# An output projection with seven quarter products for eight, and its operand's sums made one stage earlier

## The chip, the cores and the metric

The kernel runs on one core of one Trainium2 chip. The metric is the device time of one execution in microseconds (us). In the rows that are shown, PE is TensorE (matmul), PEld its weight load, DVE is VectorE, ACT is ScalarE, POOL is GpSimd and SP is SyncE, which issues most DMAs; ACT issues the rest from its own queue (ACTq).

## The reference

One layer of a streaming encoder for 1024 prompt tokens and 64 sample tokens of width 1024. Two attention branches (sb and cb) feed a gated merge and an output projection; the change touches only what stands behind the attention, in the reference's `merge`:

```python
b_sb = (o_sb.reshape(lead + (WIDTH_SB,)) * jax.nn.silu(z_sb)) @ w_proj_sb      # 512 -> 1024
b_cb = (o_cb.reshape(lead + (WIDTH_CB,)) * jax.nn.silu(z_cb)) @ w_proj_cb      # 512 -> 1024
h = jax.nn.sigmoid(g_sb) * b_sb + jax.nn.sigmoid(g_cb) * b_cb
return x + h @ w_out                                                           # 1024 x 1024
```

All is float32.

## The kernel before

TensorE works on float32 in a rounded form (fp32r). So each operand is split into a high part (a rounded copy, made by ACT) and a low part (the difference, made by DVE or POOL), and each product is three matmuls: high x high, high x low, low x high. A weight block `wraw` becomes `whi` and `wlo` in this way (`Weights.split`, L117; ACT for the high part, POOL for the low).

Every engine works through its own queue in program order, which the code writes out by hand; an instruction waits for its operands and for the buffers that it overwrites, and what stands behind it on its engine waits with it.

The stages that matter here come last. While the cb attention runs, the sb branch's projection fills TensorE; its results, times the gates, lie in `tb` (two tiles `tbt`, named x..1). Then comes the **cb projection** (`proj_units("cb")`, L822 to L875): 24 units, one for each block of 128 features (`u`, 0 to 7) and each of three token ranges (`CH`: 384, 384 and 320 columns). A unit is 12 matmuls into a PSUM tile. DVE multiplies it by the gate (L870) and adds `tb` (L871), ACT rounds the sum h to its high part (L872), and DVE and POOL in turn make the low part (L873). The order of units is `u` 0 and 1 through the three ranges, then 2 and 3, and so on.

The **output projection** (L1177 to L1202) goes over four blocks of 256 columns of `w_out` and, in each, over nine token tiles. A tile is 24 matmuls of 256 columns (8 k-slices of three), with h as the stationary operand and the weight moving; DVE adds x (L1201) and ACT's queue stores y (L1202). The tile of the 64 sample rows (`t == 8`) has high and low parts of h side by side in `hs`, so that 16 matmuls do for it, and `fold` adds the two halves.

An earlier stage of the kernel (the q and k projections, L600 to L642) already multiplies two by two blocks with seven products instead of eight; its sums of x are made by `make_t` (L326).

Of the kernel before, what the change touches and what calls it, by code (L numbers as in the profile page):

```python
# [8 lines left out]
F32 = mybir.dt.float32  # L9
# [8 lines left out]
KT = 8  # L18
# [14 lines left out]
def hybrid_step_kernel(ctx: ExitStack, tc: tile.TileContext, x_prompt, x_sample, c_sbk, c_sbv, c_cbk, c_cbv,  # L33
# [106 lines left out]
    units += [("ev_act", 5120 + 128 * j, (AF.Copy, d_g["cb"][j])) for j in range(KT)]  # L140

# [4 lines left out]
    with ExitStack() as ph:  # L146
# [178 lines left out]

        def make_t(tm, pool):  # L326

            x = lambda s, h, k, c: xhl[s][h][:, k, c * HF:(c + 1) * HF].bitcast(F32)

            def put(n, k, src):  # L330
                A.activation(tm[n][0][:, k], src, AF.Copy)
                V.tensor_tensor(out=tm[n][1][:, k], in0=src, in1=tm[n][0][:, k].bitcast(F32), op=OP.subtract)

            def sub(a, b, k):
                d = pool.tile([128, HF], F32, name="d")
                V.tensor_tensor(out=d, in0=x(0, *a[:1], k, a[1]), in1=x(0, *b[:1], k, b[1]), op=OP.subtract)
                V.tensor_tensor(out=d, in0=d, in1=x(1, *a[:1], k, a[1]), op=OP.add)
                V.tensor_tensor(out=d, in0=d, in1=x(1, *b[:1], k, b[1]), op=OP.subtract)
                return d

            def less(h, c, d, k):
                e = pool.tile([128, HF], F32, name="d")
                V.tensor_tensor(out=e, in0=x(0, h, k, c), in1=d, op=OP.subtract)
                V.tensor_tensor(out=e, in0=e, in1=x(1, h, k, c), op=OP.add)
                return e

            def sums_of(k):
                d = sub((0, 1), (0, 0), k)
                yield 0, k, d
                d = less(1, 1, d, k)  # L350
                yield 1, k, d
                yield 3, k, less(1, 0, d, k)
                yield 2, k, sub((1, 1), (0, 1), k)

            held = None
            for k in range(4):
                for got in sums_of(k):
                    if held:
                        put(*held)
                    held = got  # L360
                    yield
            put(*held)
# [385 lines left out]
    def run_fill():  # L748
# [25 lines left out]
        with tc.tile_pool(name="tbp", bufs=1, side="right") as tbp:  # L774
            g = proj_units("sb", tbp, 4)
            next(g)
            next(g)
            for i, v in enumerate(g):
                yield v
                og_step(i % 3 == 2)  # L780
# [9 lines left out]
    def hid(s, u):  # L790
        return xk(s, u) if u < 4 else late["h"][s][:, u - 4]

    def load_proj(i):
        if i < 8:
            w = w_proj_sb if i < 4 else w_proj_cb
            c = (i % 4) * 256
            W.load(("p", i), wpool, w[:, c:c + 256].rearrange("(k p) n -> p k n", p=128), [128, 4, 256])
# [24 lines left out]
    def proj_units(b, pool, ng):  # L822
        gts = {}
        order = [(2 * i + uu, ci) for i in range(KT // 2) for ci in range(3) for uu in range(2)]

        def load_g(x):
            if x < len(order):
                u, ci = order[x]
                a, e = CH[ci]
                gts[x] = pool.tile([128, 384], F32, name="gt", bufs=ng)  # L830
                A.dma_start(gts[x][:, :e - a], d_g[b][u][:, a:e])

        def sig(x):
            if b == "cb" and x < len(order):
                a, e = CH[order[x][1]]
                A.activation(gts[x][:, :e - a], gts[x][:, :e - a], AF.Sigmoid)

        for x in range(ng - 1):
            load_g(x)
# [5 lines left out]
        for x, (u, ci) in enumerate(order):  # L845
            i = u // 2 + (0 if b == "sb" else 4)
# [3 lines left out]
            cw = slice((u % 2) * 128, (u % 2) * 128 + 128)  # L850
# [269 lines left out]
    for ci in range(3):  # L1120
        load_og("cb", ci, late["y"])
        if ci == 1:
            next(g)
# [108 lines left out]
```

## Time and profile before

| | |
|---|---|
| median of three runs | 1026.25 us (1025.65 to 1027.78) |
| the profiled execution | 1026.4 us, of it 1024.6 us from the first to the last instruction |
| granted TensorE clock, mean | 0.998 |
| PE busy | 997.4 us (97%) |
| DVE, ACT, POOL busy | 620.6, 460.4 and 294.3 us |
| cb projection | about 875 to 923 us |
| output projection | about 923 to 1022 us |

A timeline row gives the start and length in us, engine, line, operation, `out<-in`, shape, and in brackets the idle time ahead of it with what ended it. The columns of the other views are told where they are shown.

### The profile page before, as it was taken

The numbers are of one execution on the slowest core, as the hardware profiler recorded it, in microseconds if no ns is written. First come the engines' busy times: TensorE is split into PE (matmuls) and PEld (weight loads), VectorE is DVE, ScalarE is ACT, GpSimd is POOL, SyncE is SP. The second block draws the span as 40 slices with busy tenths as digits, with TensorE's granted clock in tenths as the row PEclk, the third lists the DMA queues.
The fourth block names the chain that finished last, engine by engine and source line by source line (L and its number), as shares of the span: only waits on it lengthen the run. The fifth ranks groups of instructions, "written<-read, shape, count | busy, mean of one in ns | idle before, by whom it ended". The sixth has DMA issues, their size and how long they took to land.

```text
span 1024.6 us, 20312 instructions
## 1 busy us (share of the span) xinstructions
PE 997.4 (97%) x7608; PEld 951.5 (93%) x7608; DVE 620.6 (61%) x1219; ACT 460.4 (45%) x1064; POOL 294.3 (29%) x321
## 2 busy tenths in 40 slices
PE   5999999999999999999999999999999999999998
PEld 5999999999999999988898889898988898999998
DVE  5456663894354554189888877566667674674111
ACT  5544443343343433276676666544445433552000
POOL 3276662205344543211111101110102211453110
PEclk9999999999999999999999999999999999999999
DMA  6726567424555332696566554665656833654322
GB/s 221 229 97 213 181 243 260 136 89 139 173 172 170 118 97 76 177 239 183 139 165 165 151 145 127 183 193 156 177 156 204 236 100 116 202 164 146 108 94 72
DMA packets 174516, 164.22 MB, mean 160 GB/s; under 512 B 34961, under 2 KB 160785, under 8 KB 174289
## 3 DMA queue, kind: packets, MB, share of 16 engines
q1 hardware_dynamic: 157648, 145.08, 47.8%
q10 hardware_dynamic: 16768, 17.83, 5.7%
q8 instruction: 60, 0.98, 0.4%
q14 instruction: 40, 0.32, 0.1%
HBM read 104.14 MB, written 58.72 MB: 159 GB/s over the span
## 4 chain that ended last, share of the span: by engine, by line
PE 89%; DMA 3%; DVE 3%; ACT 2%; issue 1%; POOL 1%; SPq 0%; ACTq 0%; DVEq 0%; POOLq 0%
PE acc L450 18%; PE acc L755 16%; PE b L619 15%; PE acc L861 9%; PE o L1019 7%; PE pt L980 6%; PE z L929 3%; PE z L928 3%; PE acc L1197 3%; PE acc L1196 3%; PE acc L1195 3%; DVE kp L948 1%; DMA out_dram<-kos 1%; DMA wrawx<-in_w_in_dram 1%; DMA ot<-d_osb 1%
## 5 line engine op out<-in xcount | busy, mean ns | idle before, releaser
L114 POOL TENSOR_TENSOR wlo<-wraw,whi 128x1024 fp32r<-128x1024 f32 x35 | 85.6, 2445 | 281.6 <-ACT whi L107 242.7
L755 PE MATMUL acc<-xh,wlo 128*128 128x384 f32 (+1 forms) x384 | 130.7, 340 | 0.0
L755 PE MATMUL acc<-xh,whi 128*128 128x384 f32 (+1 forms) x384 | 130.2, 339 | 0.0
L755 PE MATMUL acc<-xl,whi 128*128 128x384 f32 (+1 forms) x384 | 128.6, 335 | 0.0
L948 DVE TENSOR_TENSOR_SCAN kp<-kp,imp 64x576 f32<-64x576 f32 (+8 forms) x72 | 102.7, 1427 | 21.7 <-ACT kp L931 21.5
L980 PE MATMUL pt<-ident,be 128*128 128x128 f32 (+2 forms) x608 | 89.6, 271 | 6.6 <-DVE wT L991 3.3
L938 ACT ACTIVATE be<-be,sm 128x640 f32<-128x640 f32 (+5 forms) x72 | 50.7, 704 | 95.4 <-DVE sm L934 95.4
L989 ACT ACTIVATE wT<-pt 128x512 f32<-128x512 f32 (+3 forms) x130 | 63.5, 502 | 53.2 <-PE pt L980 53.0
L980 PEld LDWEIGHTS pt<-ident,be 128*128 128x128 f32 (+2 forms) x608 | 68.7, 140 | 17.9 <-issue 6.4
L450 PE MATMUL acc<-whi,xh 128*128 128x256 f32 x256 | 74.7, 294 | 0.0
L755 PEld LDWEIGHTS acc<-xh,whi 128*128 128x128 f32 x384 | 72.7, 189 | 1.6
L755 PEld LDWEIGHTS acc<-xh,wlo 128*128 128x128 f32 x384 | 72.5, 189 | 1.1
L755 PEld LDWEIGHTS acc<-xl,whi 128*128 128x128 f32 x384 | 72.3, 188 | 0.9
L450 PE MATMUL acc<-wlo,xh 128*128 128x256 f32 x256 | 71.2, 280 | 0.0
L450 PE MATMUL acc<-wlox,xh 128*128 128x256 f32 x256 | 71.2, 280 | 0.0
L450 PE MATMUL acc<-whi,xl 128*128 128x256 f32 x256 | 71.2, 280 | 0.0
L450 PE MATMUL acc<-whix,xh 128*128 128x256 f32 x256 | 71.2, 280 | 0.0
L450 PE MATMUL acc<-whix,xl 128*128 128x256 f32 x256 | 71.1, 280 | 0.0
L949 DVE TENSOR_TENSOR be<-be,kp 64x576 f32<-64x576 f32 (+8 forms) x72 | 60.3, 837 | 9.6
L931 ACT ACTIVATE kp<-z 128x384 f32<-128x384 f32 (+6 forms) x112 | 54.2, 484 | 24.7 <-PE z L929 23.2
L1019 PE MATMUL o<-wT,vp 128*64 128x256 f32 (+1 forms) x608 | 65.2, 356 | 0.0
L1019 PEld LDWEIGHTS o<-wT,vp 128*64 128x64 f32 x608 | 41.4, 136 | 23.1 <-issue 7.1
(240 smaller groups left out, 2919.4 us busy)
## 6 DMA issues: line engine op xcount, KB each, us to landing
wraw<-in_w_in_dram SPq DMA_DIRECT2D x35, 512.0 KB, 4.3
wrawx<-in_w_in_dram SPq DMA_DIRECT2D x13, 512.0 KB, 4.4
sq<-d_qsbT SPq DMA_DIRECT2D x32, 192.0 KB, 4.6
sq<-d_qcbT SPq DMA_DIRECT2D x32, 192.0 KB, 4.1
xt<-in_x_prompt_dram SPq DMA_DIRECT2D x8, 512.0 KB, 6.1
d_kcbT<-hl SPq DMA_DIRECT2D x8, 512.0 KB, 4.5
d_qcbT<-hl SPq DMA_DIRECT2D x8, 512.0 KB, 5.1
d_ksbT<-hl SPq DMA_DIRECT2D x16, 256.0 KB, 2.6
```

The source lines that it names most:

```text
L114: (eng or G).tensor_tensor(out=l, in0=raw, in1=h[:].bitcast(F32), op=OP.subtract)
L450: TE.matmul(ps, x, w, start=m == 0, stop=m == len(steps) - 1)
L619: TE.matmul(ps[:, :m], w[:, hl_, k], right[s](x)[:, k, a:b], start=s < 3 and k == 0 and e == 0, stop=k == 3 and e == 2, skip_group_check=s ...
L755: TE.matmul(ps[:, :b - a], w[:, k], xk(x, k)[:, a:b], start=k == 0 and n == 0, stop=k == KT - 1 and n == 2)
L861: TE.matmul(ps[:, :n], w[:, p, cw], g[:, a:e], start=p == 0 and m == 0, stop=p == NPAIR - 1 and m == 2)
L931: A.activation(kp[:r, x:y], z[:r, :m], AF.Sigmoid, scale=-0.125)
L938: A.activation(be[:r, :n], be[:r, :n], AF.Exp, bias=kp[:r, j:j + 1], scale=-1.0, accum_out=kp[:r, 2:3])
L948: V.tensor_tensor_scan(kp[:r, n - 1::-1], kp[:r, n - 1::-1], im[:, ::-1], 0.0, op0=OP.mult, op1=OP.add)
L949: V.tensor_tensor(out=be[:r, :n], in0=be[:r, :n], in1=kp[:r, 1:n + 1], op=OP.mult)
L980: TE.transpose(pt[:kr, x, :r], be[:r, kb * 128:kb * 128 + kr], ident[:r, :r])
L989: A.activation(w[:, sl:sl + m, q0:q0 + r], pt[:, :m, :r], AF.Copy)
L1019: TE.matmul(o[hd * 64:hd * 64 + 64, c0:c1], vv[:kr, kb, hd * 64:hd * 64 + 64], wT[b, p, j, hd, s // 4][:kr, s % 4, c0:c1], start=si == 0, ...
```

## The change

The output projection is regrouped. `w_out` is taken as two pairs of 256-column blocks; with h cut in two by features (512 and 512) and by tokens (512 and 512), each pair is a 2 x 2 by 2 x 2 block product, done with seven quarter products. A quarter product is 4 token tiles x 4 k-slices x 3 matmuls of 256 columns. Four of the seven left operands are sums of quarters of h (`th0` to `th3`, each with a high and a low part); the four sums of weight blocks are made for each pair. The order of products is `OP_ = [0, 3, 1, 2, 4, "b", 5, 6]`, where `"b"` is a block that only the sample rows need. Products 0, 3 and 6 take h itself, product 1 takes `th1`, product 2 `th0`.

The sums of h are made during the cb projection. Its units now go in the order `u` 0 and 4, 1 and 5, 2 and 6, 3 and 7. The product with the gate stays on DVE (now L891), the addition goes to POOL for all 24 units and writes h over `tb` (L892), ACT rounds one unit later and DVE makes the low part three units later (`keep_h`, L913). From the ninth unit on, one step of `sums_h` (L923, L928) follows each unit: a subtraction of 512 columns, its rounding on ACT and its low part, for one k-slice after the other. The last k-slice's sums stand behind product 0 in the code.

The core of the diff:

```diff
-                t2 = gt
-                hh, hlo = hid(0, u)[:, a:e], hid(1, u)[:, a:e]
-                V.tensor_tensor(out=t2[:, :n], in0=ps[:, :n], in1=gt[:, :n], op=OP.mult)
-                V.tensor_tensor(out=t2[:, :n], in0=t2[:, :n], in1=tb(u)[:, a:e], op=OP.add)
-                A.activation(hh, t2[:, :n], AF.Copy)
-                (G if x % 2 else V).tensor_tensor(out=hlo, in0=t2[:, :n], in1=hh.bitcast(F32), op=OP.subtract)
-            load_g(x + ng - 1)
+                h = tb(u)
+                V.tensor_tensor(out=gt[:, :n], in0=ps[:, :n], in1=gt[:, :n], op=OP.mult)
+                G.tensor_tensor(out=h[:, a:e], in0=gt[:, :n], in1=h[:, a:e], op=OP.add)
+                keep.append((u, a, e))
+                if len(keep) > 3:
+                    keep_h(1, *keep.pop(0))
+                if len(keep) > 1:
+                    keep_h(0, *keep[-2])
+                if x > 7:
+                    next(late["t"][(x - 2) // 6 - 1], None)
+            load_to(x + ng)
...
+    def sums_h(k):
+        x = lambda h, c: tb(k + 4 * h)[:, 512 * c:512 * c + 512]
+        d = {}
+        def step(n, p, q):
+            d[n] = late["hp"].tile([128, 512], F32, name="d", bufs=2)
+            V.tensor_tensor(out=d[n], in0=p, in1=q, op=OP.subtract)
+            A.activation(late["tm"][n][0][:, k], d[n], AF.Copy)
+        def low(n):
+            h, l = (late["tm"][n][s][:, k] for s in range(2))
+            V.tensor_tensor(out=l, in0=d[n], in1=h.bitcast(F32), op=OP.subtract)
+        step(0, x(0, 1), x(0, 0))
+        step(1, x(1, 1), d[0])
+        yield
+        low(0)
+        step(3, x(1, 0), d[1])
+        yield
+        low(1)
+        step(2, x(1, 1), x(0, 1))
+        yield
+        low(3)
+        yield
+        low(2)
...
+    for _ in g:
+        pass
+    prep_o(1)
+    keep_h(0, *keep[-1])
+    while keep:
+        keep_h(1, *keep.pop(0))
...
+    load_ow((0, 0, 1), ow1, "qraw", 2)
+    load_ow((0, 1, 1), ow1, "qraw", 2)
+    for _ in late["t"][2]:
+        pass
+    t3 = late["t"][3]
...
+    for i in range(2):
...
+        for q, s in enumerate(OP_):
+            n = 8 * i + q
+            for m in {0: (), 1: (3,), 2: (4, 5)}.get(n, (n + 3,)):
+                prep_o(m)
...
+            for c in range(2) if s != "b" else ():
+                if s < 3:
+                    bank[OB[s], c] = psB.tile([128, 2, 256], F32, name=f"b{OB[s]}{c}")
+                ps = bank[OB[s], c]
+                for t in range(2):
+                    ts_ = slice((2 * c + t) * 128, (2 * c + t) * 128 + 128)
+                    for k in range(4):
+                        for e, (xs_, wt_) in enumerate(((0, wh), (1, wh), (0, wl))):
+                            TE.matmul(ps[:, t], left[s](xs_)[:, k, ts_], wt_[:, k], start=s < 3 and t == k == e == 0,
+                                      stop=k == 3 and e == 2, skip_group_check=s > 2 or t > 0)
+                p = ps[:]
+                if s == 0:
+                    A.activation(s1[c], p, AF.Copy)
+                    if n == 0 and c == 1:
+                        for _ in t3:
+                            pass
...
+            if n == 0:
+                prep_o(2, V)
```

`prep_o` splits a weight block or a sum of blocks: the sums for product 1 (`ws`) on POOL in the first pair, the high part on ACT, the low part on POOL but for product 1's of the first pair, which is DVE's (the last line). The `qraw` loads take memory that the cb projection's operand `og` held. The gate loads of the cb branch now come behind the last loads and roundings of its `og`, and go to eight buffers. Its weights are loaded as two halves of 128 columns.

DVE's queue at the end of the cb projection and the start of the output. Before, the last units (`gt` products, sums, low parts `hlo`) and then the output's y:

```order
L870 TENSOR_TENSOR gt<-acc,gt 128x384
L871 TENSOR_TENSOR gt<-gt,xl_10321 128x384
L870 TENSOR_TENSOR gt<-acc,gt 128x320
L871 TENSOR_TENSOR gt<-gt,xl_10321 128x320
L873 TENSOR_TENSOR hlo<-gt,hh 128x320
L870 TENSOR_TENSOR gt<-acc,gt 128x320
L871 TENSOR_TENSOR gt<-gt,xl_10321 128x320
L1175 COPY hs<-xl_141 128x4x64
L1175 COPY hs<-hlo 128x4x64
L1201 TENSOR_TENSOR y<-acc,xr 128x256 x4
```

Now, the last twelve rows up to the first y; ahead of them stand the last gate product and the last low parts of h. `xh_10320` and `xl_10321` are the two tiles of h, `d` is a sum of h, `th..l` its low part, `wloo` the low part of product 1's weight:

```order
L1265 TENSOR_TENSOR hs<-xl_10321,hs 128x4x64
L928 TENSOR_TENSOR th2l<-d,th2h 128x512
L923 TENSOR_TENSOR d<-xh_10320 128x512
L923 TENSOR_TENSOR d<-xl_10321,d 128x512
L928 TENSOR_TENSOR th0l<-d,th0h 128x512
L923 TENSOR_TENSOR d<-xl_10321,d 128x512
L928 TENSOR_TENSOR th1l<-d,th1h 128x512
L923 TENSOR_TENSOR d<-xl_10321,xh_10320 128x512
L928 TENSOR_TENSOR th3l<-d,th3h 128x512
L928 TENSOR_TENSOR th2l<-d,th2h 128x512
L1237 TENSOR_TENSOR wloo<-ws_12020,whio 128x1024
L1360 TENSOR_TENSOR xh_12016<-b_11948,xr 128x512
```

Between the last gate product and the first y there were two copies; now there are sixteen instructions: low parts of h, the rest of the third k-slice's sums, the whole of the fourth's, and the weight's low part.

POOL's queue over the last units. Before, low parts of h between low parts of weights:

```order
L873 TENSOR_TENSOR hlo<-gt,hh 128x320
L114 TENSOR_TENSOR wlo<-wraw,whi 128x1024
L873 TENSOR_TENSOR hlo<-gt,hh 128x384 x2
L873 TENSOR_TENSOR hlo<-gt,hh 128x320
L114 TENSOR_TENSOR wlo<-wraw,whi 128x1024
L114 TENSOR_TENSOR wlox<-wrawx,whix 128x1024
```

Now an addition for every unit, and then the two sums for product 1 (`ws_12018`, `ws_12020`) between low parts:

```order
L892 TENSOR_TENSOR xh_10320<-ot,xh_10320 128x384
L892 TENSOR_TENSOR xl_10321<-ot,xl_10321 128x384
L892 TENSOR_TENSOR xh_10320<-ot,xh_10320 128x320
L892 TENSOR_TENSOR xl_10321<-ot,xl_10321 128x320
L1237 TENSOR_TENSOR wlo<-wraw,whi 128x1024
L1220 TENSOR_TENSOR ws_12018<-qraw 128x1024
L1228 TENSOR_TENSOR ws_12020<-ws_12018,wraw 128x1024
L1237 TENSOR_TENSOR wloo<-ws_12018,whio 128x1024
```

The additions came from DVE, and the output's first weights no longer follow the low parts directly.

More of the change, by code (lines that the diff above doesn't have):

```diff
@@ new lines, in hybrid_step_kernel @@
+    late["o"] = prep_o
+    g = proj_units("cb", late["tbp"], 8)
+    for ci in range(3):
+        load_og("cb", ci, late["y"])
+        fill((40, 24, 100000)[ci])
+        if ci == 2:
+            next(g)
+            next(g)
+            late["h"][1] = [xpool.tile([128, 4, T], F32R, name=f"x{s}0") for s in "hl"]
+        make_og("cb", ci)
+    for _ in g:
[4 more added lines that the diff above has]
+        keep_h(1, *keep.pop(0))
+    m4.close()
+    late["tbx"].close()
```

345 lines of the change are left out of this document (223 added, 122 removed).

## The prediction

> **What bounds the kernel now.** I read the page first, then the busy time by stage, then the chain that ended last, and then the timelines of DVE and POOL.
>
> ```profile
> PE 997.4 (97%) x7608; PEld 951.5 (93%) x7608; DVE 620.6 (61%) x1219; ACT 460.4 (45%) x1064; POOL 294.3 (29%) x321
> 875.00:923.00 48.00, 48.00 (x294) 48.00 (x293) 35.87 (x55) 26.94 (x51) 26.23 (x18) 1.00 0.54 168
> 923.00:1022.00 99.00, 97.98 (x831) 97.58 (x829) 24.67 (x54) 12.16 (x20) 17.72 (x9) 1.00 0.34 107
> ```
>
> The first row is the whole span. The other two are stages, with columns window, length, then busy time of PE, PEld, DVE, ACT, POOL, clock, DMA share and rate. TensorE is full in both: the second branch's projection (875 to 923) and the output projection (923 to 1022). The difference is the rest: the output stage needs little of DVE and POOL, but in the projection they are busy for 35.9 + 26.2 = 62 us out of 48. The change loads that stage further.
>
> ```profile
> L861 PEld LDWEIGHTS acc<-og,whi x192: 187/188/188, 875.1 to 922.2; 128*128 128x128 f32 x192
> 922.53 0.31 PE L861 MATMUL acc<-og,wlo 128*128 128x320 f32 x1
> L1195 PE MATMUL acc<-whi,xh x128: 277/280/283, 922.7 to 1019.4; 128*128 128x256 f32 x128
> 1012.04 0.28 PE L1195 MATMUL acc<-whix,hh 128*128 128x256 f32 x1
> ...
> 1014.86 0.28 PE L1195 MATMUL acc<-whix,hh 128*128 128x256 f32 x1
> 1021.24 0.13 PE acc L1197
> 1021.39 0.42 DVE y L1201
> ```
>
> The projection's matmuls run from 875.1 to 922.65, the output's from 922.7 to 1021.37. Between the two L1195 rows lie 24 matmuls (8 k-slices of three): 2.82 / 24 = 0.1175 us each. So a matmul removed here is worth 0.1175 us as long as TensorE is not made to wait.
>
> **What the change removes.** Each output tile had 8 x 3 matmuls: 32 tiles x 24 = 768, and 64 for the sample rows. Now there are 2 pairs x 7 products x 4 tiles x 4 k-slices x 3 = 672, and still 64. That is 96 fewer: 96 x 0.1175 = **11.3 us** off TensorE.
>
> **What it adds, and the resource that it lands on.** The sums of h cost DVE 32 instructions of 512 columns (16 subtractions, 16 low parts). POOL takes over all 24 additions of the projection; DVE gets all low parts of h. POOL also makes two sums of weights before product 1 can start. The question is whether DVE and POOL can do this side by side, and the trace says no:
>
> ```profile
> 883.35 0.56 DVE L873 TENSOR_TENSOR xl<-gt,xh 128x384 fp32r<-128x384 f32 x1 [0.66 <-ACT xh L872]
> 905.35 2.40 POOL L114 TENSOR_TENSOR wlo<-wraw,whi 128x1024 fp32r<-128x1024 f32 x1
> 905.97 2.19 DVE L873 TENSOR_TENSOR hlo<-gt,hh 128x384 fp32r<-128x384 f32 x1 [1.33 <-ACT hh L872]
> 867.19 1.02 POOL L814 TENSOR_TENSOR og<-ot,og 128x384 fp32r<-128x384 f32 x1 [0.31 <-ACT og L809]
> 885.47 0.56 DVE L871 TENSOR_TENSOR gt<-gt,xh 128x384 f32<-128x384 f32 x1
> 885.60 1.30 POOL L873 TENSOR_TENSOR xl<-gt,xh 128x384 fp32r<-128x384 f32 x1 [4.33 <-ACT xh L872]
> 235.74 1.75 POOL L420 TENSOR_TENSOR whix<-ws,whix 128x512 fp32r<-128x512 f32 x1
> 236.73 0.42 DVE L627 TENSOR_TENSOR u<-b,s 128x256 f32<-128x256 f32 x1 [0.39 <-DMA wrawx<-in_w_in_dram]
> ```
>
> Alone, a DVE subtraction of 384 columns takes 0.56. The one that starts at 905.97, while POOL is inside an instruction until 907.75, ends at 908.16: 0.41 after POOL. The other way round, POOL's 384 columns take 1.02 alone and 1.30 when DVE is at work until 886.03; it ends 0.87 after that. So a DVE instruction with both operands in SBUF and a POOL instruction take turns, and each change-over saves 0.15 against end to end. The last row is no such instruction: one operand (`b`) is in PSUM, and it takes its 0.42 in the middle of a POOL instruction. The multiplications by the gate (`gt<-acc,gt`) are of that kind.
>
> The Trainium skill ("SBUF — State Buffer", section "Who interferes with whom") gives the rule: two-SBUF-input VectorE work and GpSimd work that reads SBUF share one port pair under an exclusive lock for the whole instruction. The trace agrees but for the 0.15; strictly by the rule the turn-taking sum below would end at 955.8, and the kernel at 1035.
>
> The remaining prices, each of an instruction that nothing disturbed (in the summary rows the figures are least, median and most in ns; the least is the 320-column form):
>
> ```profile
> 228.67 0.69 DVE L387 TENSOR_TENSOR ws<-wraw 128x512 f32<-128x512 f32 x1
> L871 DVE TENSOR_TENSOR gt<-gt,xh x12: 491/557/561, 882.1 to 903.1; 128x384 f32<-128x384 f32 x8, 128x320 f32<-128x320 f32 x4
> 120.36 0.42 DVE L302 TENSOR_TENSOR hl<-pk,hl 128x256 fp32r<-128x256 f32 x1 [0.42 <-ACT hl L301]
> 144.57 0.29 DVE L302 TENSOR_TENSOR hl<-pk,hl 128x128 fp32r<-128x128 f32 x1 [1.21 <-ACT hl L301]
> L114 DVE TENSOR_TENSOR wlo<-wraw,whi x1: 1215/1215/1215, 12.7 to 12.7; 128x1024 fp32r<-128x1024 f32 x1
> L870 DVE TENSOR_TENSOR gt<-acc,gt x24: 475/545/552, 881.5 to 929.4; 128x384 f32<-128x384 f32 x16, 128x320 f32<-128x320 f32 x8
> 930.99 0.88 POOL L873 TENSOR_TENSOR hlo<-gt,hh 128x320 fp32r<-128x320 f32 x1 [1.85 <-ACT hh L872]
> 879.32 1.96 POOL L814 TENSOR_TENSOR og<-ot,og 128x320 fp32r<-128x320 f32 x2
> ```
>
> **The sum that sets the end.** Product 1 of the first pair needs the third sum of h for all four k-slices and its weight's low part (DVE, `wloo<-ws,whio`). In DVE's queue that low part stands behind everything of the projection, including the whole last k-slice of sums. From 879.3 (the last low parts of og, last row above) up to and with it, the two engines must take turns for:
> - DVE: 2 low parts of og x 0.49, 12 x 0.56 + 4 x 0.42 + 4 x 0.29 low parts of h, 32 x 0.69 for the sums, 2 x 0.42 for hs, 1.22 for the weight: 34.6 us.
> - POOL: 2 x 0.88 of og, 16 x 1.02 + 8 x 0.88 additions, 7 x 2.40 of 1024 columns (five low parts of weights, two sums): 41.9 us.
>
> End to end 76.5 us, so 955.8. Each of up to 60 change-overs saves 0.15: the floor is 946.8. The 24 multiplications (16 x 0.545 + 8 x 0.48 = 12.6 us) stand in DVE's queue too; if none lay beside a POOL instruction the ceiling would be 968.4. Laying the queues out instruction by instruction with these prices I get 948 to 952, depending on who goes first when both are ready, and I take **950.5**. The same layout for the queues of before puts the last multiplication at 930.3; the trace has 929.40:
>
> ```profile
> 929.40 0.47 DVE L870 TENSOR_TENSOR gt<-acc,gt 128x320 f32<-128x320 f32 x1
> PE acc L1197 <- POOL hlo L873: 0.4, 1, 0.4
> ```
>
> The first row also shows that DVE was 6.8 us behind TensorE (922.65) already, at a cost of 0.4 us of waiting (second row, from the waits), since the first output tile needed only earlier units.
>
> Without a wait TensorE would reach product 1 after products 0 and 3 and 16 sample matmuls: 922.65 + 112 x 0.1175 = 935.8. So 14.7 us of the way it must wait, part of it already inside products 0 and 3 (their low parts stand behind the last multiplication), the rest ahead of product 1. After that 736 - 112 = 624 matmuls x 0.1175 = 73.3 us: end of TensorE 1023.8, against 1021.37.
>
> Later blocks have cover: a product takes 48 x 0.1175 = 5.6 us, a block's low part 2.4 on POOL, and blocks are split three ahead. The gate loads moved behind the branch's own og loads have the PSUM ring of six units as cover; I cost them at nothing, and up to 1 us if a late first gate holds the ring. The projection's weights come in two loads of half the columns each, two units ahead: nothing. The x loads for the first y go through SP while TensorE waits: nothing.
>
> **The tail.** The last y is 512 columns, not 256 (0.69 for 0.42), and its store 256 KB instead of 128 KB:
>
> ```profile
> out_dram<-y ACTq DMA_DIRECT2D x32, 128.0 KB, 1.9
> d_ksbT<-hl SPq DMA_DIRECT2D x16, 256.0 KB, 2.6
> ```
>
> Together +1.0 us. The profiled execution took 1026.4 (0.15 over the median of the runs): 1026.4 + (1023.8 - 1021.37) + 1.0 = **1029.8 us**. The gain of 11.3 is more than eaten by 14.7 us of waiting less the 0.4 to 1 of before. Break-even is product 1 starting at 947.1. With the floor and 953 as bounds this case gives 1026 to 1032.5.
>
> **Rivals.**
> - *TensorE's clock falls in the wait.* After 2.37 us of idle time the clock fell; after 2.89 us elsewhere it did not:
>
> ```profile
> 787.57 0.34 PE L861 MATMUL acc<-xl,whi 128*128 128x384 f32 x1
> ...
> 790.78 0.44 PE L980 MATMUL pt<-ident,be 128*128 128x128 f32 x2 [2.37 <-ACT wT L989]
> ...
> 793.03 0.53 PE L861 MATMUL acc<-xh,whi 128*128 128x384 f32 x1
> 793.35 0.53 PE L861 MATMUL acc<-xl,whi 128*128 128x384 f32 x1
> 792.00:794.00 2.00, 2.00 (x10) 2.00 (x9) 1.82 (x7) 1.39 (x4) 0.00 (x0) 0.57 0.89 256
> 257.80 0.44 PE L580 MATMUL acc<-ident,s 128*128 128x128 f32 x2 [2.89 <-ACT ko L586]
> 254.00:258.00 4.00, 1.11 (x10) 0.87 (x9) 0.10 (x1) 0.60 (x3) 1.16 (x1) 1.00 0.79 237
> ```
>
> The granted clock was 0.57, and matmuls started 0.32 apart. At half pace for some 3 us this costs 1.5 us if it falls behind product 1's start, nothing if it falls in products 0 or 3, where TensorE is early anyway. 1031.3 (1028 to 1034). The Trainium skill ("TensorE: Matmul & The Clock Gate", section "What's actually happening") says that about 3.4 us of idleness halves the clock; a wait of 4 us ahead of product 1 would then do it, an estimate of +1.7 us.
> - *The work hides, and it gets faster.* Place: DVE ahead of product 1. If turn-taking cost nothing (the sums slide into time in which DVE only waits for ACT), product 1 starts at 935.8, and the kernel takes 1026.4 + 935.8 + 73.3 - 1021.37 + 1.0 = 1015.1. It decides from a start before 945. For it: DVE and POOL now often wait for ACT (the marks `<-ACT hh` above), and the new order asks ACT a unit ahead. Against it: the 76.5 us.
> - *The output stage waits later on.* ACT's queue has stores that wait for DVE's y ahead of the next blocks' high parts. Block 4 must be split by 950.5 + 2 x 5.6 = 961.7 and I have it at 959. Should each pair lose one product's time to this: 1033 to 1040.
>
> **Chances.** Forecast 0.52, the clock 0.25, later waits 0.10, faster 0.13. About 0.2% (2 us) is what a measurement of this kernel can tell from no change: 1024.2 to 1028.3. The forecast's own spread puts 0.3 of it in that band, the clock's 0.05: same 0.17, faster 0.14, slower 0.69. The range leaves out most of the faster case and the end of the later waits: 1023 to 1036.
>
> **What would show it.** Right: the last gate multiplication ends 9 us or more behind the projection's last matmul; TensorE's idle time lies in products 0 and 3 and ahead of product 1 (first `th1h` matmul at 948 to 953), put down to DVE; DVE's 512-column rows there have a mean near 1 us instead of 0.69; from product 1 on no wait. Wrong: `th1h` starts near 936, or TensorE waits within the second pair, or the projection itself stops.

## The result: 1036.5 us, slower by 1.0%

The changed kernel takes 1036.49 us (median of 4 runs, 1034.78 to 1038.12); the kernel before took 1025.95 us beside it (4 runs, 1023.93 to 1027.78). The ratio is 1.0103, 95% interval 1.0078 to 1.0129. The forecast was 1029.8, range 1023 to 1036: the direction was right, the loss of 10.5 us is nearly three times the 3.6 forecast, and the time lies just outside the range. The profiled execution of the changed kernel took 1038.12 us, 1.6 over its median, with a span of 1036.3.

The page of the changed kernel, busy time and number of instructions of each engine over the whole span:

```profile
PE 996.2 (96%) x7512; PEld 947.9 (91%) x7512; DVE 672.3 (65%) x1246; ACT 475.6 (46%) x1088; POOL 330.1 (32%) x342
```

Its busy time by stage follows; before, two rows were enough, one for the projection and one for the output. The columns are window, length, busy time of PE, PEld, DVE, ACT and POOL, granted clock, DMA share and rate:

```profile
875.00:923.00 48.00, 47.60 (x289) 47.37 (x288) 37.86 (x50) 24.58 (x51) 29.82 (x24) 1.00 0.49 148
923.00:936.00 13.00, 6.21 (x36) 5.50 (x35) 12.93 (x15) 6.25 (x13) 7.90 (x6) 0.72 0.29 95
936.00:950.00 14.00, 12.33 (x89) 11.83 (x89) 13.97 (x14) 4.87 (x10) 9.53 (x5) 0.89 0.13 42
950.00:960.00 10.00, 4.88 (x28) 4.47 (x27) 8.62 (x14) 4.80 (x7) 2.47 (x1) 0.83 0.16 53
960.00:1000.00 40.00, 40.00 (x338) 40.00 (x337) 23.35 (x24) 10.79 (x12) 22.93 (x9) 1.00 0.48 154
1000.00:1036.00 36.00, 32.38 (x272) 32.17 (x270) 16.16 (x22) 3.94 (x5) 8.16 (x3) 0.98 0.33 106
```

The 96 matmuls are gone (7608 to 7512). TensorE is still full in the projection (875 to 923) and again from 960. Between them lie 37 us in which it works for 23.4, while DVE is busy for 12.93 of 13, 13.97 of 14 and 8.62 of 10 us. The granted clock is 0.72 to 0.89 there. The waits of TensorE in that stretch follow: what it waited for, us in total, times, and the longest in us:

```profile
PE b L1337 <- ACT whio L1236: 4.4, 1, 4.4
PE b L1337 <- DVE h0l L913: 4.3, 1, 4.3
PE b L1337 <- POOL wlo L1237: 2.4, 2, 1.8
PE b L1337 <- ACT s L1341: 1.0, 1, 1.0
PE b L1337 <- DVE wloo L1237: 0.8, 1, 0.8
PE b L1337 <- ACT h0h L911: 0.7, 1, 0.7
```

Together they are 13.6 us, all in products 0 and 3 and at product 1's first matmuls; there are none later. The timeline shows where they come from:

```profile
875.76 5.06 ACTq L842 DMA_DIRECT2D gt<-d_gcb  x4
882.09 2.40 POOL L114 TENSOR_TENSOR wlo<-wraw,whi 128x1024 fp32r<-128x1024 f32 x1 [5.29 <-ACT whi L107]
925.08 0.31 PE L883 MATMUL b<-og,wlo 128*128 128x320 f32 x1
938.97 0.48 DVE L891 TENSOR_TENSOR ot<-b,ot 128x320 f32<-128x320 f32 x1
945.95 2.45 POOL L1228 TENSOR_TENSOR ws<-ws,wraw 128x1024 f32<-128x1024 f32 x1
946.07 2.61 DVE L1265 TENSOR_TENSOR hs<-xh,hs 128x256 fp32r<-128x256 f32 x1
955.31 1.23 DVE L1237 TENSOR_TENSOR wloo<-ws,whio 128x1024 fp32r<-128x1024 f32 x1 [0.26 <-ACT whio L1236]
955.33 0.39 PE L1337 MATMUL b<-whio,th1h 128*128 128x256 f32 x1 [4.36 <-ACT whio L1236]
956.59 0.58 PE L1337 MATMUL b<-wloo,th1h 128*128 128x256 f32 x1 [0.76 <-DVE wloo L1237]
1032.10 0.28 PE L1337 MATMUL b<-wloo,xh 128*128 128x256 f32 x1
```

The projection's last matmul ends at 925.39, the last multiplication by the gate 14.1 us later, at 939.45; it was 7.0 us later before. A DVE instruction of 256 columns, 0.42 us when undisturbed, takes 2.61 here (`hs<-xh,hs`): it ends 0.28 us behind the POOL instruction beside it. The low part ahead of it on DVE, 256 columns too, takes 2.62 beside the POOL instruction ahead. Product 1's operand and weights are ready at 956.5. The longest wait in the list, put down to ACT (`whio`), goes back to DVE: ACT rounds that block of weights in its queue only behind its roundings of the sums, the last of which DVE makes up to 953.7.

### The profile page after: what moved, and what is told of

Its sections match the earlier page's. It is cut to its first block, busy times and chain, and to the rows that moved or that the text cites. A ratio compares the mean times of both kernels' runs of the same rounds, so it can differ in the third digit from the quotient of the medians.

```text
span 1036.3 us, 20146 instructions
## 1 busy us (share of the span) xinstructions
PE 996.2 (96%) x7512; PEld 947.9 (91%) x7512; DVE 672.3 (65%) x1246; ACT 475.6 (46%) x1088; POOL 330.1 (32%) x342
## 4 chain that ended last, share of the span: by engine, by line
PE 87%; DVE 6%; DMA 3%; issue 1%; ACT 1%; POOL 1%; SPq 0%; ACTq 0%; DVEq 0%; POOLq 0%
PE acc L453 18%; PE acc L758 17%; PE b L622 15%; PE o L1085 7%; PE b L1337 7%; PE pt L1046 6%; PE acc L883 6%; PE z L995 3%; PE z L994 3%; PE b L883 2%; DVE kp L1014 1%; DMA out_dram<-kos 1%; DMA wrawx<-in_w_in_dram 1%; DVE be L1015 1%; PE pk L338 1%
## 5 line engine op out<-in xcount | busy, mean ns | idle before, releaser
L114 POOL TENSOR_TENSOR wlo<-wraw,whi 128x1024 fp32r<-128x1024 f32 x31 | 75.9, 2449 | 257.0 <-ACT whi L107 220.8
L453 PE MATMUL acc<-wlo,xh 128*128 128x256 f32 x256 | 71.2, 280 | 0.0
L453 PE MATMUL acc<-wlox,xh 128*128 128x256 f32 x256 | 71.2, 280 | 0.0
L453 PE MATMUL acc<-whi,xl 128*128 128x256 f32 x256 | 71.2, 280 | 0.0
L453 PE MATMUL acc<-whix,xh 128*128 128x256 f32 x256 | 71.2, 280 | 0.0
```

The lines of the kernel that those rows point to most:

```text
L114: (eng or G).tensor_tensor(out=l, in0=raw, in1=h[:].bitcast(F32), op=OP.subtract)
L453: TE.matmul(ps, x, w, start=m == 0, stop=m == len(steps) - 1)
```

## The experiments

There are two theories on why product 1 is late. **A**: DVE instructions with both operands in SBUF and POOL's instructions take turns, as forecast. **B**: DVE's own queue is too long, and POOL has nothing to do with it. Later the question became what is left when the turns are shortened. In the diffs, `V` is DVE, `G` POOL and `A` ACT. Each time is a median; the ratio is against the kernel before, run on the same chip in between. It is these ratios that are compared, since the kernel before itself moved between 1025.95 and 1027.85 from one set of runs to the next. Where a gain is given in us, it is a difference of medians; by the ratios the gains against the changed kernel differ from that by 0.2 to 0.9 us. The profiled executions also differ in when the projection ends (925.39 in the changed kernel). Where that moves a figure, the text says by how much.

### e1: the sums' differences in PSUM

```
-            d[n] = late["hp"].tile([128, 512], F32, name="d", bufs=2)
+            d[n] = late["psB"].tile([128, 512], F32, name=f"b{3 if k == 3 else 1}{len(d) % 2}")
```

> The differences d of the sums stand in PSUM banks that are free at that time (those of product 1's group 1 for the first three row blocks, those of group 3 for the last) instead of SBUF. The 32 instructions on DVE, their order and POOL's are unchanged; 24 of the 32 (all but steps 0 and 2) now have only one operand in SBUF. Theory A (DVE with two operands in SBUF and POOL take turns): these 24 can run inside POOL's instructions, so product 1 starts 6 to 10 us earlier than its 955.3, the DVE rows of 512 columns fall from 1.4 to about 0.7, and the time is 1026 to 1030. Rival B (DVE's own queue is the limit and POOL doesn't matter): the same instructions take the same time, 1035 to 1038.

Measured 1032.83 us, ratio 1.0065 (1.0043 to 1.0087). That is a smaller gain than A said and a larger one than B said. The durations settle between them. By source line, first the changed kernel, then this run (least, median and most in ns, then first and last start):

```profile
L923 DVE TENSOR_TENSOR d<-xh x4: 679/1489/1505, 897.2 to 949.5; 128x512 f32<-128x512 f32 x4
L923 DVE TENSOR_TENSOR d<-xl,d x8: 691/692/1390, 898.7 to 951.6; 128x512 f32<-128x512 f32 x8
L928 DVE TENSOR_TENSOR th0l<-d,th0h x4: 693/1498/1510, 901.3 to 950.9; 128x512 fp32r<-128x512 f32 x4
```

```profile
L923 DVE TENSOR_TENSOR b<-xh x4: 683/1502/1507, 896.2 to 941.5; 128x512 f32<-128x512 f32 x4
L923 DVE TENSOR_TENSOR b<-xl,b x8: 695/696/697, 899.6 to 948.8; 128x512 f32<-128x512 f32 x8
L928 DVE TENSOR_TENSOR th0l<-b,th0h x4: 681/682/683, 901.2 to 948.0; 128x512 fp32r<-128x512 f32 x4
```

And TensorE's two waits in the timeline of this run:

```profile
932.98 0.55 PE L1337 MATMUL b<-whi,h0h 128*128 128x256 f32 x1 [9.21 <-DVE th3l L928]
941.65 0.38 PE L1337 MATMUL b<-whi,h0h 128*128 128x256 f32 x1 [3.22 <-DVE th2l L928]
```

In the second table `b` is the PSUM bank that holds the difference. The `xh` row of each is the one difference whose two operands come from the same tile of h in SBUF, in either kernel: median 1.49 and 1.50 us, no change. The other two rows have one operand in PSUM now: the low parts of `th0` fall from a median of 1.50 to 0.68, and no instruction of the two rows is longer than 0.70. In the timelines three of these four low parts lie wholly inside a POOL instruction. Order and POOL's work are the same, so it is where the operand stands that decides, and B falls. The timeline says why so little came of it: product 0 now waited 12.4 us for its own PSUM banks, in which row block 2's differences stood.

### e2: the additions on DVE

```
-                G.tensor_tensor(out=h[:, a:e], in0=gt[:, :n], in1=h[:, a:e], op=OP.add)
+                V.tensor_tensor(out=h[:, a:e], in0=gt[:, :n], in1=h[:, a:e], op=OP.add)
```

> The 24 additions of the projection go from POOL to DVE, operands in SBUF as before. Theory A: 24 x (1.02 - 0.56) = 11 us of turns go away, but the gate multiplications (24 x 0.48), which ran inside POOL's instructions, now stand in one queue with everything else; of the 11 us about 1 to 3 are left: 1033 to 1036. Rival B (DVE's queue alone is the limit): DVE gets 24 x 0.56 = 13.4 us more and product 1 starts later by most of it: 1043 to 1050.

Measured 1034.53, ratio 1.0086 (1.0061 to 1.0111). DVE got 24 instructions more, some 13 us of undisturbed work, and the kernel did not get slower; B's 1043 to 1050 is out. DVE's busy time on the page is even a little less, 671.2 us for 672.3: the additions took the place of time that its instructions had spent waiting for POOL's. A's 1 to 3 us are there as a median (2.0), though the intervals of the two kernels overlap.

### e3: no additions

```
-                G.tensor_tensor(out=h[:, a:e], in0=gt[:, :n], in1=h[:, a:e], op=OP.add)
+                G.tensor_tensor(out=h[:, a:a + 1], in0=gt[:, :1], in1=h[:, a:a + 1], op=OP.add)
```

> The 24 additions on POOL are cut to one column each (the first branch's value is left out of the others). Theory A: POOL's share of the turns falls by up to 24 x (1.02 - 0.15) = 21 us, product 1 waits no longer for the sums but at most for its weights, PE loses 2 to 5 us in place of 13.6: 1024 to 1029. Rival B: DVE's instructions are all still there and product 1 starts when it did: 1034 to 1038.

This kernel leaves the sum of the two branches out, but for one column of each unit; it only prices the additions, each of which still takes 0.18 to 0.44 us (0.15 in the expectation). Measured 1024.09, ratio 0.9975 (0.9960 to 0.9989), at the fast end of A's range; TensorE's waits are 4.4 us for 13.6. The low part of product 1's weights in the timeline, the row to compare with 955.31:

```profile
942.26 1.23 DVE L1237 TENSOR_TENSOR wloo<-ws,whio 128x1024 fp32r<-128x1024 f32 x1 [0.25 <-ACT whio L1236]
```

It came 13.05 us earlier, of which 0.12 is the projection's end, with every DVE instruction of the sums and low parts still there. So POOL's 24 additions cost the end 12.4 us (13.1 by the ratios), though POOL is busy for only 32% of the span.

### e4: gate loads that do not hold ACT

```
+                gts[x] = (late["hp"].tile([128, 512], F32, name="d", bufs=2) if b == "cb" and x < 2 else
...
-        load_to(min(ng - 1, 4))
+        load_to(2 if b == "cb" else ng - 1)
...
         sig(0)
+        load_to(min(ng - 1, 4))
```

> The second branch's first two gate loads get buffers that nobody else uses, and the next two are issued behind the split of the projection's second weight block, so ACT no longer stands 5.06 us in the gate loads ahead of that split. Theory D (the late begin of the turns, POOL's first instruction at 882.1 instead of 879.3, is a part of the loss): product 1 starts 2 to 3 us earlier, 1033 to 1035. Theory A alone, with the turns full anyway and the begin given back: 1036 to 1037.

Measured 1037.23, ratio 1.0108 (1.0087 to 1.0129): no gain, and a little above A's range. POOL's first instruction of the stage and product 1's weights in its timeline:

```profile
877.81 2.39 POOL L114 TENSOR_TENSOR wlo<-wraw,whi 128x1024 fp32r<-128x1024 f32 x1 [1.70 <-ACT whi L107]
953.37 1.22 DVE L1239 TENSOR_TENSOR wloo<-ws,whio 128x1024 fp32r<-128x1024 f32 x1 [0.26 <-ACT whio L1238]
```

The turns begin 4.3 us earlier (877.81 for 882.09) and product 1's weights are ready 1.9 us earlier, of which 0.7 is the projection's end in either case. Nothing of it reaches the time. Theory D falls: ACT holds the begin of the turns up, but that is not what the kernel loses by.

### e5: the same differences, in banks that are free

```
-            d[n] = late["hp"].tile([128, 512], F32, name="d", bufs=2)
+            d[n] = (late["psF"].tile([128, 512], F32, name="acc") if k == 2 else
+                    late["psB"].tile([128, 512], F32, name=f"b{3 if k == 3 else 1}{len(d) % 2}"))
```

> As the run with the differences in PSUM, but in banks that no product is about to need: row block 2 takes the two accumulators that the projection no longer uses, row blocks 0 and 1 product 0's banks, row block 3 product 2's. In the first run PE waited 9.2 and 3.2 us ahead of products 0 and 3 for these banks. Theory A with the banks as the reason for the small gain: product 0 waits only for the low parts of h (last one for it at 932.2 there), ACT is not held by product 0's copies, and the low part of product 1's weights ends 4 to 5 us earlier than that run's 953.7: 1027 to 1030. Rival: the waits for banks only covered the waits behind POOL's three weight instructions (2.4 us each), which remain: 1031 to 1033.

Measured 1029.78, ratio 1.0029 (1.0017 to 1.0042), at the slow end of what A expected. Product 1's weights in the timeline:

```profile
946.86 1.23 DVE L1238 TENSOR_TENSOR wloo<-ws,whio 128x1024 fp32r<-128x1024 f32 x1 [0.25 <-ACT whio L1237]
```

The weights' low part begins 8.45 us earlier than in the changed kernel (955.31), of which 2.7 is the projection's end (922.70), and the time falls by 6.7. Without e1's waits for banks its gain of 3.7 us is nearly doubled, as A expected.

### e6 and e7: product 2 ahead of product 1

```
-    OP_ = [0, 3, 1, 2, 4, "b", 5, 6]
+    OP_ = [0, 3, 2, 1, 4, "b", 5, 6]
...
+                        next(t3)
+                        prep_o(2, V)
                         for _ in t3:
```

> Operands in SBUF as in the changed kernel, but product 2 is made ahead of product 1: it needs one of POOL's two weight sums and two of the eight instructions that the last row block's sums take on DVE (one difference, one low part), and its weights' low part stands third among them. Theory A, where DVE's queue ahead of the product sets its start: of eight instructions of 0.69 behind 949.5 only three stand ahead of the low part of the weights, product start 3 to 3.5 us earlier (952 to 953): 1032.5 to 1034. Rival C (the start is set by POOL's weight sums or ACT): POOL's first sum ends at about 946, not late, so no more is gained; if ACT's queue sets it, 1036 to 1037.

Measured 1033.43, ratio 1.0068 (1.0053 to 1.0083): 3.1 us less than the changed kernel, inside A's 1032.5 to 1034. The weights of the first product that needs sums, in the timeline:

```profile
951.16 1.23 DVE L1240 TENSOR_TENSOR wloo<-ws,whio 128x1024 fp32r<-128x1024 f32 x1 [0.98 <-ACT whio L1239]
```

It begins 4.15 us earlier, of which 1.5 is the projection's end, with five instructions of the sums behind it that stood ahead of it. Next come e5's banks (but row block 3 in product 1's) with this order:

> Differences in PSUM (row block 3 in product 1's banks) and product 2 ahead of product 1. Theory A: the gains of the two runs beside this one add up but for a microsecond, since both shorten DVE's queue ahead of the first product that needs sums: 1024 to 1028, and PE's idle time behind the projection falls from 13.6 to 5 us or less. Rival: products 0 and 3 wait for the low parts of h behind POOL's instructions as before, and that alone keeps it at 1029 to 1032.

Measured 1027.45, ratio 1.0012 (0.9993 to 1.0030): by the medians the two gains add up to within a microsecond (6.7 + 3.1 = 9.8 hoped for, 9.0 measured), by the ratios only to within two (11.2 and 9.3), which the intervals allow. The kernel is level with the one before. TensorE still waited 3.2 us in product 0 and 2.7 at product 2.

### e8: matmuls in the wait

```
+            if n == 1:
+                scr = psF.tile([128, 512], F32, name="acc")
+                for z in range(28):
+                    TE.matmul(scr[:, :256], h1[0][:, 0, 0:128], wh[:, 0], start=z == 0, stop=z == 27)
```

> The changed kernel with 28 more matmuls of 256 columns (28 x 0.1175 = 3.3 us) between product 3 and product 1, into an accumulator that is not read, in the 4.4 us in which PE waited. Theory C (the half clock that follows the wait costs time): the clock in the window 955 to 960 is full, 0.8 us of waiting for the weights' low part stays, 1034 to 1035.5. Rival (the half clock costs nothing that shows, since product 1 waits anyway for other things): 1036 to 1037.5.

Measured 1036.01, ratio 1.0090 (1.0071 to 1.0108). The time lies in the rival's range, but this tells nothing apart: 1.8 us of the waits ahead of product 1 stayed, and the clock fell all the same. In the busy time by stage it is 0.66 from 955 to 960, in this run and in the changed kernel alike; this run's row:

```profile
955.00:960.00 5.00, 5.00 (x30) 5.00 (x31) 3.68 (x6) 0.38 (x1) 2.05 (x1) 0.66 0.39 123
```

No run shows by itself what the half clock costs.

### e9 and e10: less ahead of the products

e9 takes e7, moves the split of the sample rows (`hs`) and their products behind product 2, and makes a row block's second difference one tile later. e10 also takes the sums of row block 2 out of the projection.

```
+            if n == 2:                      # e9: sample products of pair 0 here, not at n == 1
+                prep_o(4)
+                prep_o(5)
...
-                    next(late["t"][(x - 2) // 6 - 1], None)
+                    next(late["t"][(x - 2) // 6 - 1], None) if x < 20 else None      # e10
```

> As the run with both changes (1027.45), and the sample rows' split (two instructions on DVE that stood 2.5 us each behind POOL's weight sums) and their products go behind the first product that needs sums; the second difference of a row block is made one tile later, so that DVE doesn't wait 1.9 us for ACT at it. Theory A: the wait of 1.9 and 0.8 us ahead of the third product goes and that of 3.2 us in product 0 falls to about 1.5: 1022 to 1024.5. Rival: the third product's weights wait for POOL's first weight sum and ACT, not for DVE, and the idle time stays: 1026 to 1028.

> As the run beside this one, and the sums of row block 2 are made behind the low parts of h instead of among them. Theory A: DVE's queue ahead of product 0 loses some 5 us (7 instructions of 0.7), product 0 waits for nothing, and the eight instructions of the two row blocks that the third product needs not are hidden by it: 1021 to 1024. Rival: the work that moved behind comes due ahead of the third product and PE waits there instead, 1024 to 1027.

e9 measured 1024.44, ratio 0.9986 (0.9971 to 1.0000), at the end of A's range; e10 measured 1027.16, ratio 1.0011 (0.9998 to 1.0024), a miss for A. In e10 product 0 ran without a wait, and then, in its timeline:

```profile
932.61 0.60 ACT L925 ACTIVATE th0h<-acc 128x512 fp32r<-128x512 f32 x1 [5.27 <-DVE acc L924]
935.36 0.60 ACT L925 ACTIVATE th0h<-b 128x512 fp32r<-128x512 f32 x1 [2.15 <-DVE b L924]
935.85 1.08 ACT L1344 ACTIVATE s<-b 128x512 f32<-128x512 f32 x2
936.50 0.58 PE L1340 MATMUL b<-whi,xh 128*128 128x256 f32 x1 [7.66 <-ACT s L1344]
```

The copies of product 0 (`s`) stood in ACT's queue behind two roundings that waited for DVE, which took turns with POOL's weight sums. Product 3 accumulates into the bank that is copied, and waited 7.7 us for it.

### e11 to e14: the waits that are left, one after the other

e11 is e10 with the copies ahead of the roundings, both weight sums on DVE and product 1's weights rounded earlier; e12 moves `hs` ahead of the second weight sum; e13 holds the sums of row blocks 2 and 3 in one bank each and makes product 4's weights' low part on DVE; e14 puts the sample products between the halves of product 2.

```
-                eng2 = G if n < 8 else V
+            eng2 = V                                            # e11
...
+                        prep_o(2, V)
+                            A.activation(hs[:, u, 0:64], f, AF.Copy)      # e12; in e11 behind the sums
+                        prep_o(3)
+                        for _ in range(4):
+                            next(t2, None)
+                            next(t3, None)
...
+                d[n] = d[0] if d else late["psB"].tile([128, 512], F32, name=f"b2{k - 2}")   # e13, k > 1
...
+                if n == 2 and c == 0:                           # e14
+                    samples(i, 0, *first)
+                    samples(i, 3, *second)
```

> As the run with row block 2 behind the low parts of h, where PE waited 7.7 us ahead of product 3 for a copy that stood in ACT's queue behind the rounding of a difference that DVE could not make (it stood behind POOL's two weight sums): the copies go ahead of the roundings, DVE makes the two weight sums (1.21 each for POOL's 2.5), and product 1's weights are rounded ahead of the sums that come due later. Theory A: product 3 waits at most 1 us, product 2's weights' low part ends at 935 to 937, and PE is idle 1 to 3 us behind the projection: 1019 to 1022, below the kernel before. Rival: work on DVE is the limit behind the projection whatever takes turns (some 17 instructions of 0.4 to 1.2 us between 926 and 945), and products 2 and 1 wait for it: 1023 to 1026.

> As the run before it, in which PE's one long wait behind the projection was 4.5 us for the split of the sample rows, which stood at the end of DVE's queue, ahead of the sample products behind product 2: the split goes ahead of the second weight sum and of the sums that come due later (0.84 us more ahead of these). Theory A (PE is late only by what stands ahead in the queues): the wait goes, product 1's operand (then at about 945.7) is there when the sample products end (about 946.2), and the time is 1019 to 1021.5. Rival: the sums that moved behind by 0.84 us are late for product 1 by as much or more, and the clock falls again in that wait: 1022.5 to 1024.5.

> As the run before it, in which PE still waited 2.5 us ahead of the sample products for an accumulator in which row block 2's differences stood, and 1.5 us ahead of product 4 for the low part of its weights from POOL. Row blocks 2 and 3 now keep their four differences one after another in a single bank each (both of product 1's group), so the accumulators are free, and DVE makes that low part (1.21 for 2.4). Theory A (what is left behind the projection is waits that the queues and banks make): 3 to 4 us go, 1020 to 1022. Rival E (the kernel is at PE's floor but for the clock, and a wait removed here comes back at the next product, whose operand is finished last): 1023 to 1025.

> As the run before it, in which the waits that were removed came back as 3.0 us ahead of product 4, whose weights are prepared behind the sample products (DVE waits at these products' sums before it makes product 4's weights). The sample products go between the two halves of product 2, 2.8 us earlier, and with them the preparation of product 4's weights. Theory A (waits that queues make): product 4's wait goes from 3.0 to 1 or less, and with it the fall of the clock behind it: 1021 to 1023.5. Rival E (DVE's instructions are still all there and the last of them is late for some product): the wait moves to product 1 or 4 again, 1024 to 1026.

| run | us | ratio to before | 95% interval |
|---|---|---|---|
| e11 | 1024.68 | 0.9980 | 0.9967 to 0.9993 |
| e12 | 1024.42 | 0.9987 | 0.9978 to 0.9996 |
| e13 | 1025.85 | 0.9991 | 0.9979 to 1.0004 |
| e14 | 1023.85 | 0.9973 | 0.9957 to 0.9988 |

By their intervals e11, e12 and e14 beat the kernel before, by 0.1 to 0.3%; among the four the intervals overlap, so they can't be ranked. Theory A's ranges were missed each time, by 2.7, 2.9, 3.9 and 0.4 us. TensorE's longest waits behind the projection, from the timelines of e11, e12, e13 and e14, in this order; for e14 with three rows of DVE:

```profile
948.80 0.58 PE L1383 MATMUL acc<-whi,hs 128*128 128x256 f32 x1 [4.51 <-DVE hs L1357]
```

```profile
944.86 0.55 PE L1383 MATMUL acc<-whi,hs 128*128 128x256 f32 x1 [2.54 <-ACT th2h L925]
955.91 0.39 PE L1339 MATMUL b<-wlo,th2h 128*128 128x256 f32 x1 [1.47 <-POOL wlo L1242]
```

```profile
944.73 0.39 PE L1350 MATMUL b<-whio,th1h 128*128 128x256 f32 x1 [1.28 <-DVE th2l L931]
953.72 0.35 PE L1350 MATMUL b<-whi,th2h 128*128 128x256 f32 x1 [2.98 <-ACT whio L1252]
```

```profile
941.67 0.38 PE L1369 MATMUL b<-whio,th1h 128*128 128x256 f32 x1 [1.29 <-DVE th2l L931]
950.68 0.55 PE L1369 MATMUL b<-whi,th2h 128*128 128x256 f32 x1 [2.99 <-ACT whio L1252]
945.58 0.42 DVE L1336 TENSOR_TENSOR fl<-acc,fl 64x256 f32<-64x256 f32 x1 [2.00 <-ACT fl L1335]
946.37 1.21 DVE L1244 TENSOR_TENSOR xl<-wraw,qraw 128x1024 f32<-128x1024 f32 x1
949.85 1.28 DVE L1397 TENSOR_TENSOR xh<-b,s 128x512 f32<-128x512 f32 x2
```

Each wait that was taken away came back at a later product: the rows shown are 4.5, 4.0, 4.3 and 4.3 us in sum, the whole lists 5.0, 4.8, 5.6 and 4.8. In e14 the wait at product 4 is the same as in e13, although its preparation was moved half a product (2.8 us) ahead in the code. Product 4's weights (`xl`, 946.37) stand on DVE behind the sample rows' sum (`fl`), and that waits for ACT, whose queue has the stores and loads of the first y ahead of it. Product 4 also writes into the bank of product 1, which DVE reads (L1397) only behind the low part of these weights: the first of the two readings ends at 950.53, 0.15 us ahead of product 4's first matmul. The trace puts the wait down to a rounding on ACT that ends at 950.57 and that product 4 does not use by the code, so which of the two released it is not shown. So rival E holds in its effect, but its reason, DVE's work alone, is only half of it: it is a chain through the queues of DVE and ACT.

## Why the prediction came out as it did

- **The 96 matmuls: right.** There are 7512 for 7608, and no wait behind product 1's first three matmuls; the rival with waits later in the output stage did not happen.
- **The mechanism: right, and shown.** The gate multiplications fall behind (14.1 us, where the sign asked for 9 or more). The 32 instructions of 512 columns have a mean of 1.05 us, "near 1" as forecast. The waits lie in the products where they were put, 13.6 us in sum; the list puts only 5.1 of them down to DVE by name, and the longest of the others goes back to DVE through ACT's queue. e1 shows that it is the operand in SBUF, e2 that DVE's queue alone is not the cause, e3 what POOL's additions cost. The rival in which the work hides is out.
- **The step that failed: "I take 950.5" for product 1's start.** The low part of its weights is ready at 956.54 and the matmul that takes it starts at 956.59, 6.1 us later than forecast (the first `th1h` matmul is at 955.33, where the sign said 948 to 953). Of that, 2.5 us stand in this profiled execution before the stage begins: its projection ends at 925.39, that of before at 922.84. In the other runs here it ends between 920.32 and 925.95, so this is not put down to the change. The other 3.6 us belong to the step. Its sum of turns was not too small: from POOL's first instruction (882.09) to the end of `wloo` (956.54) are 74.4 us, of which 68.3 are turns and 6.1 are gaps in which neither engine is inside such an instruction (both added up over the timelines). The gaps were sized wrong. The step takes 71.2 us (950.5 - 879.3), 3.7 above its floor of 67.5; the trace has 74.4, 6.9 above it: 0.8 of turns and 6.1 of gaps. They are mostly 0.3 to 0.6 us each, in which DVE makes a gate multiplication or waits for ACT while POOL waits for DVE. So a good part of the 12.6 us of multiplications did not lie beside POOL. The turns also begin 0.2 us later than the projection's end explains.
- **The price by the strict rule.** By the strict rule of the Trainium skill ("SBUF — State Buffer", section "Who interferes with whom") the prediction had the kernel at 1035, nearer to the result. No row here bears the rule out in that strictness: the change-overs do overlap (68.3 us of turns where end to end gives 76.5). That the time came out near it is luck: the gaps, the start of this execution and the clock made up the difference.
- **"The gate loads: at nothing, up to 1 us": wrong in the trace, without weight in the time.** They held ACT for 5.06 us, and POOL behind it; e4 took that away and gained nothing that can be measured.
- **The 73.3 us behind product 1's start: 2.5 short.** From 956.59 to the last matmul's end at 1032.38 are 75.8 us. More than half of it is the rival with the clock, which the prediction had priced at 1.5 us and kept apart from the forecast: the granted clock was 0.50 from 957 to 959 (the row is in the last section). In the 3.4 us up to 960 start 17 matmuls, 2.0 us' worth, so 1.4 us are lost there. The other 605 start 0.1194 us apart on average instead of 0.1175, which is 1.3 us with the end of the last; two had been made before 956.59, 0.2 us the other way. That the fall of the clock costs this much is read from the rows; e8 could not show it.
- **The tail: +0.7 for +1.0.** From the last matmul's end to the end of the execution are 1038.12 - 1032.38 = 5.74 us; before, they were 1026.40 - 1021.37 = 5.03.
- **The sum.** 6.1 + 2.5 - 0.3 = 8.3 us lead from 1029.8 to 1038.1 for the profiled execution. Against the median the miss is 6.7, since this execution lies 1.6 above it.

It is open what the rest of the 11.3 us goes to in the best versions: e14 keeps 4.0 us of it against the kernel before by the medians, 2.8 by the ratio. Its waits behind the projection are 4.8 us in the list, but their price together with the clock was not measured by itself.

## What to carry to other kernels

Before moving work from DVE to POOL, count POOL's instructions and those of DVE with both operands in SBUF as one queue; here 24 additions on an engine that was busy for 32% of the span cost the kernel 12.4 us. If an intermediate can be kept in PSUM, the DVE instruction that reads it leaves that queue at no cost in time of its own, but look at who needs the bank next (in e1 product 0 waited 12.4 us for that). When waits follow one another, look for the work or the chain behind them, not only at the wait that shows: three reorderings in a row (e12 to e14) moved some 4 us from product to product.

## What the runs showed of the hardware

- A DVE instruction with one operand in SBUF and the other in PSUM takes 0.68 to 0.70 us for 512 columns wholly inside a POOL instruction, as when alone, with the result in SBUF (e1) or in PSUM (`b<-xl,b` in e9). With both operands in SBUF it takes up to 1.5 beside POOL's additions and 2.8 beside its weight sums (e10), even with the result in PSUM.
- With the difference in PSUM, DVE's next reader of it began only when ACT had read it. The changed kernel's timeline has ACT's rounding and DVE's next difference, which read the same tile in SBUF, start together; the group of that line in e1 has 11.0 us of idle time ahead of it, in four places (the columns behind the bars are busy time and mean in ns, then idle time and what ended it):

```profile
950.25 0.63 ACT L924 ACTIVATE th0h<-d 128x512 fp32r<-128x512 f32 x1 [7.70 <-DVE d L923]
950.25 0.69 DVE L923 TENSOR_TENSOR d<-xl,d 128x512 f32<-128x512 f32 x1
```

```profile
L923 DVE TENSOR_TENSOR b<-xl,b 128x512 f32<-128x512 f32 x8 | 5.6, 696 | 11.5 <-ACT th0h L924 11.0
```

  Whether the chip needs this order or only the built program asks for it was not tried.
- The clock did not wait for a single long pause. In the changed kernel TensorE waited 1.76 us up to 927.38, 0.74 up to 929.22 and 4.29 up to 934.10, with seven matmuls between the first two and one between the last two. In the busy time by stage the clock is 0.95 from 927 to 929 and 0.50 for ten us from there, although the longest of these waits began only at 929.81 and TensorE worked through the second five. So the 3.4 us of idleness that the prediction cites were not needed here. In e8 the clock fell behind waits of 1.07 and 0.75 us; in e13, behind one of 2.98 us, it was 0.75 on average over five us. The rows are those of the changed kernel, then that of e13:

```profile
927.00:929.00 2.00, 1.10 (x7) 0.90 (x7) 2.00 (x2) 0.35 (x1) 1.61 (x2) 0.95 1.05 367
929.00:934.00 5.00, 0.58 (x1) 0.29 (x1) 4.97 (x9) 2.59 (x6) 2.47 (x3) 0.50 0.15 51
934.00:939.00 5.00, 4.90 (x23) 4.90 (x24) 4.93 (x8) 1.74 (x5) 2.03 (x2) 0.50 0.00 0
957.00:959.00 2.00, 2.00 (x11) 2.00 (x11) 1.11 (x3) 0.38 (x1) 1.77 (x1) 0.50 0.48 152
```

```profile
955.00:960.00 5.00, 5.00 (x35) 5.00 (x34) 2.86 (x4) 1.06 (x1) 5.00 (x3) 0.75 1.03 329
```
